# Merging weight pieces of seven-product pairs, two raw buffers plus one by stage, and a seventh seven-pair in an attention kernel

## The chip, the cores and the metric

The kernel runs on one core of one Trainium2 chip. The metric is device time in microseconds (us). The kernel before was timed in three runs: 2825.72, 2826.1 and 2832.35 us, with the median at 2826.1.

## The reference

Two layers on x of 512 rows (S) by 2048 columns (D), in float32, batch 1:

```python
def reference(x, c, ...):
    for l in range(2):
        mod = silu(c) @ ada_w[l] + ada_b[l]           # shift, scale, gate
        h = rmsnorm(x, g_pre[l]) * (1 + scale) + shift
        if l == 0:
            y = mlstm_mixer(h, a_w_in, ...)           # 8 heads, then @ a_w_out
        else:
            hkv = rmsnorm(x, kv_g) * (1 + kscale) + kshift
            k, v = split(hkv @ kv_w)                  # 2048 -> 2 x 2048
            y = band_attention_mixer(h, k, v, b_w_in, b_rel, b_w_out)
        x = x + gate * rmsnorm(y, g_post[l])
```

The first mixer projects h to queries, keys, values (8 heads of 512), an output gate o and a gate z, runs a gated linear attention over the heads, and multiplies by a_w_out (4096 to 2048). The second projects h to queries q and gates z for 16 heads of 128, takes a softmax over scores with a learned bias by relative position, mixes the values, multiplies by silu(z), and multiplies by b_w_out (2048 to 2048).

## The kernel before

Every large product is made as three matmuls of split operands (`mm3`, L215): each float32 value is split into a high and a low part (`split`: the high part cast on ACT, L179, the low part subtracted on DVE, L180), and TensorE (PE) adds hi x hi, hi x lo and lo x hi in PSUM (L213). Activations are kept in SBUF as such pairs. Weights are streamed in pieces, in the order of a list (`stream`), by `wpiece` (L184): one DMA on SP's queue into a tile `raw` of up to 128 x 1024 floats (`wr`, 512 KB), then `wh` on ACT and `wl` on DVE. Pool `wp` has three buffers each of raw, hi and lo. Pieces are numbered over the whole stream (wr0, wr1, ...).

`proj_s` (L255) makes two output column blocks of 128 at once, over pairs of row blocks k. A pair is handled in one of two ways. An "eight" is the plain product: 12 matmuls of 512 columns. A "seven" is one level of a Strassen-like scheme: seven products of 256 columns, 21 matmuls, for which sums of the weights are made first: `ws` in three DVE steps on raw (L199 to L201), split into `wsh` and `wsl`. It also needs sums of the activations (`half_sums`, `three_sums`), made by `head_sums` for the first layer and `input_sums` for the second. `pair_pieces(f)` sets what goes into a piece: of eight pairs, f are sevens. The first pieces hold one seven and one eight (1024 columns); the remaining sevens go one to a piece of 512 columns (256 KB), or, for kv_w, two to a piece.

The stages, in the trace's time: modulation, norm and leading projections until 240 us; heads 0 to 3 until about 820; heads 4 to 7, in which o and z are made by `proj_s` with five sevens of eight pairs, until about 1530; the product with a_w_out (`ps_y`), until about 1898; values (`ps_kv`) and keys of the second layer, with the residual of the first layer beside them, until about 2235; 16 attention heads (`queries`, `weights`, `flipped`, `mixed`) until about 2635, one every 25.46 us; the product with b_w_out (`ps_y` of y1) and the last norm. At the start of the head called HALF, the fourth counted from 0, a pool is closed and another, `hq`, opened for the sums; the values v of that head are evicted from PSUM (pool psP, 5 banks) by ACT and DVE in between.

A scheduler sets the order on each engine, by dependencies, priorities and pools. `tc.high_priority(300)` draws pieces and evictions ahead. An engine works strictly in that order, SP's DMA queue too: a DMA that waits for its buffer holds up all behind it. A new pool lies on memory of closed ones, so its first writes wait for the last readers there.

In the attention, head h's queries are made while head h-1's scores and softmax (`ps_s`, L990 to L993) and head h-2's mixing (`ps_o`, L1021) run at the point `mid`, in the middle of `proj_s`; `flipped` (`ps_t`) follows. After head 15's queries come the tails of heads 14 and 15. Each result z is stored to `y2c` in DRAM; the output stage loads it back in pairs as `y2r` into raw tiles of pool wp (L1060), splits it, and multiplies.

Of the kernel before, what the change touches and what calls it, by code (L numbers as in the profile page):

```python
# [15 lines left out]
P = 128  # L16
# [16 lines left out]
AHEAD = 300  # L33

# [8 lines left out]
HEAD_PAIRS = 5  # L43
HALF = NH // 2
ATT_PAIRS = 6


def pair_pieces(f, step=1):


    sk, nk = list(range(f)), list(range(f, KT // 2))
    n = min(len(sk), len(nk))
    out = [([a], [b]) for a, b in zip(sk, nk)]
    out[1:1] = [([], nk[i : i + 2]) for i in range(n, len(nk), 2)]
    return out + [(sk[i : i + step], []) for i in range(n, len(sk), step)]


def stream():
# [14 lines left out]
    def tile_s(mat, c1, c2, f, step=1):  # L73
        for sk, nk in pair_pieces(f, step):
            blocks = [(2 * k + i, c, P) for i, c in ((0, c1), (0, c2), (1, c2), (1, c1)) for k in sk]
            out.append((mat, blocks + [(2 * k + i, c, P) for k in nk for i in range(2) for c in (c1, c2)]))
# [6 lines left out]
    for h in range(NH):  # L83
# [7 lines left out]
        if h >= HALF:  # L91
            for i in range(4):
                tile_s("a_w_in", O0 + h * DV + i * P, Z0 + h * DV + i * P, HEAD_PAIRS)
# [11 lines left out]
    for i in range(KT // 2):  # L105
        tile_s("kv_w", 2 * i * P, (2 * i + 1) * P, KEY_PAIRS[i], 2)
# [24 lines left out]
def hybrid_trunk(ctx, tc, xT, xN, c, adaT, cols, wst, wg, ext, kc, out):  # L131
# [50 lines left out]
    ahead = [0]  # L182

    def wpiece(mat, ns=0, pl=None, bufs=2):  # L184
# [7 lines left out]
        with tc.high_priority(ahead[0]):  # L192
            raw = wp.tile([P, 1024], F32, tag="raw", name=f"wr{i}")[:, :n]
            nc.sync.dma_start(raw, wst[at : at + P * n].rearrange("(p n) -> p n", p=P))
            out = []
            if ns:
                w = ns * P
                t = pl.tile([P, 3 * w], F32, tag="ws", name=f"ws{i}", bufs=2)
                nc.vector.tensor_tensor(t[:, : 2 * w], raw[:, w : 3 * w], raw[:, : 2 * w], op=ALU.subtract)  # L199
                nc.vector.tensor_tensor(raw[:, w : 2 * w], t[:, w : 2 * w], raw[:, :w], op=ALU.add)  # L200
                nc.vector.tensor_tensor(t[:, 2 * w :], raw[:, 3 * w : 4 * w], raw[:, w : 2 * w], op=ALU.subtract)  # L201
# [3 lines left out]
            if ns:  # L205
                sh = pl.tile([P, 3 * w], F32R, tag="wsh", name=f"wsh{i}", bufs=bufs)
                sl = pl.tile([P, 3 * w], F32R, tag="wsl", name=f"wsl{i}", bufs=bufs)
                split(sh, sl, t)
                return hi, lo, sh, sl
        return hi, lo  # L210
# [9 lines left out]
    def proj(mat, xs, pss, nk, k0, k1, last, t0=0, t1=S, first=None):  # L220

        g = len(pss)
        for ka in range(k0, k1, nk):
            hi, lo = wpiece(mat)
# [9 lines left out]
    def proj_b(mat, xs, pss, ms=range(4), kts=KT, at={}, late=0):  # L234
# [3 lines left out]
        for k0 in range(0, kts, 2):  # L238
            if k0 in at:
                at[k0]()  # L240
            held.append((k0, *wpiece(mat)))
# [13 lines left out]
    def proj_s(mat, xs, ss, f, z1, z2, name, pl, bufs, at={}, step=1):  # L255
# [3 lines left out]
        pieces = pair_pieces(f, step)  # L259
        begun = set()  # L260
        h0, h1_ = slice(0, 256), slice(256, 512)
        for i, (sk, nk) in enumerate(pieces):
            if i in at:
                at[i]()
            ns = len(sk)
            parts = wpiece(mat, ns, pl, bufs)

            def acc(ps, cols, b, x, last):
                start = id(ps) not in begun
                begun.add(id(ps))  # L270
                hi, lo = parts[:2] if b >= 0 else parts[2:]
                w0 = (b if b >= 0 else b + 3 * ns) * P
                w = slice(w0, w0 + P)
                mm3(ps[:, cols], hi[:, w], lo[:, w], x[:, 0, :], x[:, 1, :], start, last)

            def eight():
                for m, k in enumerate(nk):
                    for j in range(2):
                        for t, ps in enumerate((A, B)):
                            acc(ps, slice(0, S), 4 * ns + 4 * m + 2 * j + t, xs[2 * k + j], False)  # L280

            def seven():
                end = i == len(pieces) - 1
                for ps, cols, b0, x, last in (
                    (D, h1_, ns, lambda k: ss[k][1], False),
                    (D, h0, 0, lambda k: xs[2 * k][:, :, h0], end),
                    (C, h0, -2 * ns, lambda k: ss[k][2], False),
                    (C, h1_, -3 * ns, lambda k: ss[k][0], end),
                    (A, h0, 3 * ns, lambda k: xs[2 * k + 1][:, :, h0], False),
                    (A, h1_, -ns, lambda k: xs[2 * k + 1][:, :, h1_], end),  # L290
                    (B, h0, 2 * ns, lambda k: ss[k][3], end),
                ):
                    if i == 0 and ps is B:
                        eight()
                    for j, k in enumerate(sk):
                        acc(ps, cols, b0 + j, x(k), last and j == ns - 1)
# [3 lines left out]
            seven()  # L300
# [60 lines left out]
    sp = st.enter_context(pool("start"))  # L361
# [100 lines left out]
    bp = mst.enter_context(pool("ada1", side="right"))  # L462
# [110 lines left out]
    def pair(c, name):  # L573
        z1, z2 = (acp.tile([P, 2, 256], F32, tag="so", name=f"{name}_{i}", bufs=6) for i in range(2))
        proj_s("a_w_in", h1, h1s, HEAD_PAIRS, z1, z2, name, hq, 2)
# [32 lines left out]
    for h in range(NH):  # L608
# [49 lines left out]
        if h == HALF:  # L658
            head_sums()
# [87 lines left out]
    rp = rst.enter_context(pool("rp", bufs=12, side="right"))  # L747
# [151 lines left out]

    with tc.high_priority(AHEAD):  # L900
        residual(2)
        residual(3)
    for pair, ms in enumerate(PAIRS):
        for g in range(2):
# [3 lines left out]
            values(g, ms, turn)  # L908
    rst.close()
# [233 lines left out]
```

## Time and profile before

| what | number |
| --- | --- |
| profiled execution, its own time | 2828.65 us |
| its span | 2826.9 us |
| mean granted PE clock | 0.997 |
| median of three runs (lowest, highest) | 2826.1 us (2825.72, 2832.35) |
| weight loads of 512 KB, 384 KB, 256 KB | 466, 16, 138 |
| PE, DVE, ACT busy, share of the span | 99%, 73%, 47% |

In the rows that are quoted below, a timeline row gives the start in us, the length in us, the engine, the line, the operation, output and inputs, shape, and a count (x2: two in a row, merged). A bracket at the end tells how long the engine stood idle before, and what ended it. Starts are what to subtract: lengths of pipelined matmuls overlap. PEclk is the clock that was granted to PE, as a share of the full one. A waits row gives the total, the number of times and the longest.

### The profile page before, as it was taken

How to read it: one execution, taken by the hardware profiler on the slowest of the kernel's cores; microseconds unless marked ns; L12 is line 12 of the kernel's file. 1: busy time of each engine (PE TensorE's matmuls, PEld its weight loads, DVE VectorE, ACT ScalarE, POOL GpSimd, SP SyncE). 2: the span in 40 equal slices, each digit the busy share in tenths (PEclk: the TensorE clock that was granted, in tenths of full speed). 3: DMA queues.
4: the chain of work that ended last, by engine and by line, in shares of the span. 5: the costliest groups of instructions: out<-in, count | busy, mean ns of one | idle time of the engine just before them, and what ended most of it. 6: DMA issues, size and time to landing. Idle time of an engine off the chain costs nothing.

```text
span 2826.9 us, 40577 instructions
## 1 busy us (share of the span) xinstructions
PE 2788.7 (99%) x15173; PEld 2417.6 (86%) x15173; DVE 2050.1 (73%) x3668; ACT 1337.0 (47%) x2040; POOL 0.2 (0%) x4
## 2 busy tenths in 40 slices
PE   7999999999999999999999999999999999999998
PEld 5787888888888989989888888888998899999887
DVE  7986978878688776766857445567985688888625
ACT  4234524234234554544635344468534466666523
POOL 0000000000000000000000000000000000000000
PEclk9999999999999999999999999999999999999999
DMA  8875687878774332332323656788535534334634
GB/s 296 300 256 179 230 313 237 298 237 282 263 245 136 98 125 85 105 105 97 116 86 135 217 198 212 251 264 283 176 130 186 157 120 128 118 126 124 222 110 171
DMA packets 184606, 524.09 MB, mean 185 GB/s; under 512 B 19620, under 2 KB 37060, under 8 KB 183896
## 3 DMA queue, kind: packets, MB, share of 16 engines
q1 hardware_dynamic: 184408, 521.49, 55.1%
q8 instruction: 119, 1.95, 0.3%
q14 instruction: 79, 0.65, 0.1%
HBM read 487.81 MB, written 38.85 MB: 186 GB/s over the span
## 4 chain that ended last, share of the span: by engine, by line
PE 89%; DVE 4%; DMA 3%; ACT 2%; issue 1%; SPq 0%; DVEq 0%; ACTq 0%
PE ps_y L213 17%; PE ps_v L213 10%; PE ps_o L213 6%; PE ps_z L213 5%; PE ps_azo L213 4%; PE ps_qk L213 4%; PE ps_az L213 4%; PE ps_kv L213 4%; PE ps_l L213 3%; PE ps_bzo L213 3%; PE ps_bz L213 3%; PE ps_dz L213 2%; PE ps_cz L213 2%; PE ps_s L213 2%; PE ps_czo L213 2%; PE ps_dzo L213 2%
## 5 line engine op out<-in xcount | busy, mean ns | idle before, releaser
L179 ACT CAST wh<-wr 128x1024 fp32r<-128x1024 f32 (+3 forms) x640 | 595.8, 932 | 833.3 <-PE ps_y L213 230.3
L180 DVE TENSOR_TENSOR wl<-wr,wh 128x1024 fp32r<-128x1024 f32 (+3 forms) x640 | 687.4, 1075 | 390.2 <-ACT wh L179 384.3
L213 PE MATMUL ps_y<-wh,y 128*128 128x512 f32 x1536 | 475.9, 390 | 0.0
L213 PEld LDWEIGHTS ps_y<-wh,y 128*128 128x128 f32 x1536 | 288.3, 188 | 59.3
L213 PE MATMUL ps_v<-wh,h 128*128 128x512 f32 x1024 | 321.7, 390 | 0.0
L179 ACT CAST wsh<-ws 128x384 fp32r<-128x384 f32 (+1 forms) x238 | 131.1, 551 | 356.3 <-issue 171.1
L213 PE MATMUL ps_y<-wl,y 128*128 128x512 f32 x768 | 299.3, 390 | 0.0
L180 DVE TENSOR_TENSOR wsl<-ws,wsh 128x384 fp32r<-128x384 f32 (+1 forms) x238 | 143.3, 603 | 154.1 <-ACT wsh L179 154.0
L213 PEld LDWEIGHTS ps_v<-wh,h 128*128 128x128 f32 x1024 | 192.3, 188 | 40.3 <-DVE zq L306 0.9
L213 PE MATMUL ps_v<-wl,h 128*128 128x512 f32 x512 | 199.9, 390 | 0.0
L370 DVE CUSTOM_DVE_ANT_0 ada<-ada,scB,cl 128x1024 f32<-128x1024 f32 x128 | 163.9, 1281 | 23.4 <-DMA ada<-in_adaT 23.2
L370 DVE CUSTOM_DVE_ANT_0 ada<-ada,scB,mod 128x1024 f32<-128x1024 f32 x128 | 164.0, 1281 | 21.6 <-DMA ada<-in_adaT 20.1
L213 PEld LDWEIGHTS ps_y<-wl,y 128*128 128x128 f32 x768 | 144.2, 188 | 29.9 <-DVE wl L180 0.5
L213 PE MATMUL ps_kv<-wh,hkv 128*128 128x512 f32 x512 | 160.6, 393 | 1.0 <-ACT wh L179 1.0
L199 DVE TENSOR_TENSOR ws<-wr 128x256 f32<-128x256 f32 (+1 forms) x238 | 106.1, 452 | 35.3 <-DMA wr<-in_wst 34.1
L213 PE MATMUL ps_qk<-h,wh 128*128 128x512 f32 x384 | 119.1, 390 | 0.0
L213 PE MATMUL ps_o<-h,wh 128*128 128x512 f32 x384 | 118.3, 389 | 0.0
L213 PE MATMUL ps_z<-h,wh 128*128 128x512 f32 x384 | 118.2, 389 | 0.0
L213 PEld LDWEIGHTS ps_kv<-wh,hkv 128*128 128x128 f32 x512 | 96.6, 189 | 21.1 <-ACT wh L179 1.4
L213 PEld LDWEIGHTS ps_v<-wl,h 128*128 128x128 f32 x512 | 96.2, 188 | 19.7 <-issue 0.9
L213 PE MATMUL ps_l<-h,wh 128*128 128x512 f32 x320 | 99.1, 391 | 2.5 <-ACT oz L456 2.0
L213 PE MATMUL ps_kv<-wl,hkv 128*128 128x512 f32 x256 | 100.6, 393 | 0.8 <-DVE wl L180 0.8
(385 smaller groups left out, 5865.3 us busy)
## 6 DMA issues: line engine op xcount, KB each, us to landing
wr<-in_wst SPq DMA_DIRECT2D x466, 512.0 KB, 4.0
ada<-in_adaT SPq DMA_DIRECT2D x256, 512.0 KB, 5.9
wr<-in_wst SPq DMA_DIRECT2D x138, 256.0 KB, 2.7
xt<-nsc SPq DMA_DIRECT2D x44, 256.0 KB, 4.1
yr<-ysc SPq DMA_DIRECT2D x16, 512.0 KB, 4.3
wr<-in_wst SPq DMA_DIRECT2D x16, 384.0 KB, 5.4
bsc<-in_ext SPq DMA_DIRECT2D x16, 320.0 KB, 5.7
xt<-in_xT SPq DMA_DIRECT2D x4, 1024.0 KB, 7.1
```

What stands on the lines that cost most here:

```text
L179: nc.scalar.copy(hi, src)
L180: nc.vector.tensor_tensor(lo, src, hi.bitcast(F32), op=ALU.subtract)
L199: nc.vector.tensor_tensor(t[:, : 2 * w], raw[:, w : 3 * w], raw[:, : 2 * w], op=ALU.subtract)
L213: nc.tensor.matmul(ps, a, b, start=start, stop=stop)
L370: pin(nc.vector.tensor_tensor_reduce(at, at, scB[:, j * D // 2 : (j + 1) * D // 2], 1.0, mod[:, i : i + 1] if j else col(CB + i), ALU.mult ...
```

## The change

The numbers of pieces fall. `pair_pieces` puts two remaining sevens into one piece of 1024 columns, as two groups with sums of their own (`ws545_0`, `ws545_1`), where it put one into 512 columns; kv_w keeps its wide group. ATT_PAIRS goes from 6 to 7, so a head's queries take 4 pieces where they took 6, and `mid` is at piece 2. Raw tiles of pool wp are two in place of three. Every third piece (its number divisible by three) takes a third raw tile in a pool that belongs to the stage, `spare[0]`: at the start `sp`, then `bp`, none from HALF to head 7, then `rp` for the first output product and the values, none for keys and attention, and pool `x2` in the output stage. `wsh` and `wsl` of the first layer have three buffers. The first pair of HALF has four sevens (RAMP), and the fifth `head_sums` moves from behind the values to piece 1 of that pair. The residual of rows 2 and 3 loses its high priority. Over the program PE's order has 8446 matmuls of 512 columns for 8626, and 6210 of 256 for 5895.

```diff
+RAW_BUFS = 2
...
+RAMP = [4, 5, 5, 5]
 HALF = NH // 2
-ATT_PAIRS = 6
+ATT_PAIRS = 7
...
     sk, nk = list(range(f)), list(range(f, KT // 2))
-    n = min(len(sk), len(nk))
-    out = [([a], [b]) for a, b in zip(sk, nk)]
-    out[1:1] = [([], nk[i : i + 2]) for i in range(n, len(nk), 2)]
-    return out + [(sk[i : i + step], []) for i in range(n, len(sk), step)]
+    n = len(nk)
+    assert n <= f
+    out = [([[a]], [b]) for a, b in zip(sk, nk)]
+    return out + [([sk[i : i + 2]] if merged else [[k] for k in sk[i : i + 2]], []) for i in range(n, f, 2)]
...
-            raw = wp.tile([P, 1024], F32, tag="raw", name=f"wr{i}")[:, :n]
+            own = spare[0] and i % (RAW_BUFS + 1) == 0
+            raw = (spare[0] if own else wp).tile([P, 1024], F32, tag="raw", name=f"wr{i}", bufs=1 if own else RAW_BUFS)[:, :n]
...
+            for j, ns in enumerate(groups):
                 w = ns * P
-                t = pl.tile([P, 3 * w], F32, tag="ws", name=f"ws{i}", bufs=2)
...
+                r = raw[:, c0 : c0 + 4 * w]
+                t = pl.tile([P, 3 * w], F32, tag="ws", name=f"ws{i}_{j}", bufs=tbufs)
...
-    sp = st.enter_context(pool("start"))
+    sp = spare[0] = st.enter_context(pool("start"))
...
-    bp = mst.enter_context(pool("ada1", side="right"))
+    bp = spare[0] = mst.enter_context(pool("ada1", side="right"))
...
+            spare[0] = None
             mst.close()
...
-        if h == HALF:
-            head_sums()
...
-                o, sz = pair_oz = pair(O0 + h * DV + i * P, f"zo{h}_{i}")
+                f = HEAD_PAIRS if h > HALF else RAMP[i]
+                o, sz = pair(O0 + h * DV + i * P, f"zo{h}_{i}", f, {1: head_sums} if len(h1s) == f < HEAD_PAIRS else {})
...
-    rp = rst.enter_context(pool("rp", bufs=12, side="right"))
+    rp = spare[0] = rst.enter_context(pool("rp", bufs=12, side="right"))
...
-                raw = wp.tile([P, 2, S], F32, tag="raw", name=f"yr{h}_{q}")
+                raw = wp.tile([P, 2, S], F32, tag="raw", name=f"yr{h}_{q}", bufs=RAW_BUFS)
...
-    with tc.high_priority(AHEAD):
-        residual(2)
-        residual(3)
+    residual(2)
+    residual(3)
...
+    spare[0] = None
     rst.close()
...
-        proj_s("b_w_in", h2, h2s, ATT_PAIRS, z[:, 0:2, :], z[:, 2:4, :], f"z{h}", kq, 3, {3: mid})
+        proj_s("b_w_in", h2, h2s, ATT_PAIRS, z[:, 0:2, :], z[:, 2:4, :], f"z{h}", kq, 3, {2: mid})
...
-    rp = ost.enter_context(pool("x2", bufs=8))
+    rp = spare[0] = ost.enter_context(pool("x2", bufs=8))
...
-            raw = wp.tile([P, 2, S], F32, tag="raw", name=f"y2r{i}")
+            raw = wp.tile([P, 2, S], F32, tag="raw", name=f"y2r{i}", bufs=RAW_BUFS)
```

The order of the instructions moves at three places. The first is DVE at the start of head 4 (HALF), around the eviction of its first block of values, v4_0, out of PSUM. h1r4 and h1s4 belong to the fifth head_sums, h1r3 and h1s3 to the fourth. Before:

```order
L569 TENSOR_TENSOR h1r4_0_6900<-h1_8_929 128x512
L319 TENSOR_TENSOR h1r3_1_6816<-h1r3_1_6816 128x256
L180 TENSOR_TENSOR h1s3_0_6822<-h1r3_0_6814,h1s3_0_6822 128x512
L316 TENSOR_TENSOR h1r4_0_6900<-h1r4_0_6900 128x256
L180 TENSOR_TENSOR h1s3_1_6825<-h1r3_1_6816,h1s3_1_6825 128x512
L569 TENSOR_TENSOR h1r4_1_6902<-h1_9_971 128x512
L180 TENSOR_TENSOR v4_0_6914<-ps_v4_0_6544,v4_0_6914 128x512
L180 TENSOR_TENSOR wl180_7032<-wr180_7025,wh180_7031 128x1024
```

And now:

```order
L182 TENSOR_TENSOR v4_0_6900<-ps_v4_0_6544,v4_0_6900 128x512
L182 TENSOR_TENSOR h1s3_1_6825<-h1r3_1_6816,h1s3_1_6825 128x512
L206 TENSOR_TENSOR ws181_0_7074<-wr181_7072 128x256
L615 TENSOR_TENSOR e4_0_6703<-e4_0_6703,p4_3_6867 128x128
L207 TENSOR_TENSOR wr181_7072<-ws181_0_7074,wr181_7072 128x128
L182 TENSOR_TENSOR v4_1_6903<-ps_v4_1_6545,v4_1_6903 128x512
L182 TENSOR_TENSOR wl180_7032<-wr180_7025,wh180_7031 128x1024
L208 TENSOR_TENSOR ws181_0_7074<-wr181_7072 128x128
L182 TENSOR_TENSOR v4_2_6906<-ps_v4_2_6546,v4_2_6906 128x512
L182 TENSOR_TENSOR wsl181_0_7083<-ws181_0_7074,wsh181_0_7082 128x384
L580 TENSOR_TENSOR h1r4_0_6964<-h1_8_929 128x512
L580 TENSOR_TENSOR h1r4_1_6966<-h1_9_971 128x512
```

The first steps of h1r4 stood ahead of v4_0 and wl180; now they stand behind v4_0, v4_1, v4_2, wl180 and the sums of piece 181.

The second is DVE at the start of the values (the first piece is 424 before and 402 now, so 430 before is 408 now). y3_2 and y3_3 are the residual's last steps; they read xr3_2 and xr3_3, which come by DMA. Before:

```order
L180 TENSOR_TENSOR wl428_16158<-wr428_16155,wh428_16157 128x1024
L779 RECIPROCAL rsn_106<-rsn_106 128x1
L789 SCALAR_TENSOR_TENSOR y3_2_15622<-y3_2_15622,rsn_106,xr3_2_16066 128x512
L180 TENSOR_TENSOR wl429_16176<-wr429_16173,wh429_16175 128x1024
L789 SCALAR_TENSOR_TENSOR y3_3_16017<-y3_3_16017,rsn_106,xr3_3_16072 128x512
L777 TENSOR_REDUCE rsn_106<-ssq_105 128x1
L180 TENSOR_TENSOR wl430_16194<-wr430_16191,wh430_16193 128x1024
```

And now:

```order
L800 SCALAR_TENSOR_TENSOR y3_1_15174<-y3_1_15174,rsn_106,xr3_1_15911 128x512
L182 TENSOR_TENSOR wl407_16027<-wr407_16024,wh407_16026 128x1024
L182 TENSOR_TENSOR wl408_16045<-wr408_16042,wh408_16044 128x1024
L182 TENSOR_TENSOR wl409_16063<-wr409_16060,wh409_16062 128x1024
L182 TENSOR_TENSOR wl410_16121<-wr410_16118,wh410_16120 128x1024
L800 SCALAR_TENSOR_TENSOR y3_2_15473<-y3_2_15473,rsn_106,xr3_2_15917 128x512
L800 SCALAR_TENSOR_TENSOR y3_3_15868<-y3_3_15868,rsn_106,xr3_3_15923 128x512
L182 TENSOR_TENSOR wl411_16139<-wr411_16136,wh411_16138 128x1024
```

The low parts of pieces 408 to 410 stood behind y3_3 (as 430 to 432); now they stand ahead of y3_2.

The third is the change from the attention to the output stage. On PE, ps_t14, ps_o14, ps_s15 belong to the tails of heads 14 and 15, and ps_y1_0 is the first row of the output product. Before, from the end of head 14's transposes:

```order
L213 MATMUL ps_y1_0_0_24928<-wl600_24935,y2_0_0_24940 128x512
L213 MATMUL ps_y1_0_0_24928<-wh600_24934,y2_0_0_24940 128x512
L213 MATMUL ps_y1_0_1_24929<-wh600_24934,y2_0_0_24940 128x512
L213 MATMUL ps_y1_0_1_24929<-wl600_24935,y2_0_0_24940 128x512
L1003 MATMUL ps_t14_3_24807<-kcs_99,s14_3_24658 128x128
L213 MATMUL ps_y1_0_1_24929<-wh600_24934,y2_0_0_24940 128x512
L213 MATMUL ps_y1_0_0_24928<-wh600_24934,y2_0_1_24943 128x512
L213 MATMUL ps_y1_0_2_24930<-wh600_24934,y2_0_0_24940 128x512
L213 MATMUL ps_o14_24814<-pt14_0_24791,vv14_24811 128x512 x3
L213 MATMUL ps_o14_24814<-pt14_1_24798,vv14_24811 128x384
L213 MATMUL ps_y1_0_2_24930<-wl600_24935,y2_0_0_24940 128x512
L213 MATMUL ps_y1_0_2_24930<-wh600_24934,y2_0_0_24940 128x512
```

And now, at the same place:

```order
L1014 MATMUL ps_t14_2_24748<-kcs_99,s14_2_24573 128x128
L1014 MATMUL ps_t14_2_24748<-kcs_99,s14_3_24582 128x128
L1014 MATMUL ps_t14_3_24754<-kcs_99,s14_3_24582 128x128
L223 MATMUL ps_o14_24761<-pt14_0_24738,vv14_24758 128x512 x3
L223 MATMUL ps_o14_24761<-pt14_1_24745,vv14_24758 128x384 x3
L223 MATMUL ps_o14_24761<-pt14_2_24751,vv14_24758 128x256 x3
L223 MATMUL ps_s15_0_24775<-kv15_24082,z15_24423 128x128
L223 MATMUL ps_o14_24761<-pt14_3_24756,kv14_23741 128x128
L223 MATMUL ps_s15_1_24782<-k15_24727,q15_24723 128x256 x3
```

The matmuls of ps_y1_0 have gone from between the tails' steps. The first of them, which reads wh546, now stands right behind the last matmul of ps_o15.

On SP at the same place, y2c7 are the stores of the results of heads 14 and 15, y2r the loads of results, x2 the loads of the residual for the last norm. Before:

```order
L194 DMA wr602_25008<-in_wst 128x1024
L1060 DMA y2r2_25014<-y2c2_92 128x1024
L194 DMA wr603_25046<-in_wst 128x1024
L1060 DMA y2r3_25052<-y2c3_93 128x1024
L1022 DMA y2c7_97<-z14_24148 128x512
L194 DMA wr604_25084<-in_wst 128x1024
L1060 DMA y2r4_25090<-y2c4_94 128x1024
L194 DMA wr605_25122<-in_wst 128x1024
L1060 DMA y2r5_25128<-y2c5_95 128x1024
L194 DMA wr606_25160<-in_wst 128x1024
L1022 DMA y2c7_97<-z15_24481 128x512
```

And now:

```order
L1033 DMA y2c7_97<-z15_24423 128x512
L199 DMA wr546_24879<-in_wst 128x1024
L1062 DMA x2_0_0_24858<-xsc_74 128x1024
L1062 DMA x2_0_1_24859<-xsc_74 128x1024
L1062 DMA x2_1_0_24862<-xsc_74 128x1024
L199 DMA wr549_24993<-in_wst 128x1024
L1062 DMA x2_1_1_24863<-xsc_74 128x1024
L1062 DMA x2_2_0_24866<-xsc_74 128x1024
L1062 DMA x2_2_1_24867<-xsc_74 128x1024
L1062 DMA x2_3_0_24870<-xsc_74 128x1024
L199 DMA wr552_25107<-in_wst 128x1024
L1062 DMA x2_3_1_24871<-xsc_74 128x1024
```

wr546 is the first piece of the output stage, in its own raw tile; it stands behind the store of z15, and so do wr549, wr552 and the x2 loads, behind which the loads y2r2 and y2r3 follow. Pieces 547 and 548 and the loads y2r0 and y2r1 stand ahead of the stores.

More of the change, by code (lines that the diff above doesn't have):

```diff
@@ L204, in wpiece @@
             split(hi, lo, raw)
-            if ns:
-                sh = pl.tile([P, 3 * w], F32R, tag="wsh", name=f"wsh{i}", bufs=bufs)
-                sl = pl.tile([P, 3 * w], F32R, tag="wsl", name=f"wsl{i}", bufs=bufs)
+            out = [(hi, lo)]
+            for j, t in enumerate(ts):
+                sh = pl.tile(list(t.shape), F32R, tag="wsh", name=f"wsh{i}_{j}", bufs=bufs)
+                sl = pl.tile(list(t.shape), F32R, tag="wsl", name=f"wsl{i}_{j}", bufs=bufs)
                 split(sh, sl, t)
-                return hi, lo, sh, sl
-        return hi, lo
+                out.append((sh, sl))
+        return out
     def mm(ps, a, b, start, stop):
@@ L223, in proj @@
         for ka in range(k0, k1, nk):
[L224 removed]
+            [(hi, lo)] = wpiece(mat)
             for k in range(ka, ka + nk):
```

84 lines of the change are left out of this document (44 added, 40 removed).

## Prediction

> **What bounds the kernel now.** I read the page's engine totals, then the chain that ended last, then the windows with a low granted clock, then the timeline around each of PE's waits.
>
> ```profile
> span 2826.9 us, 40577 instructions
> PE 2788.7 (99%) x15173; PEld 2417.6 (86%) x15173; DVE 2050.1 (73%) x3668; ACT 1337.0 (47%) x2040; POOL 0.2 (0%) x4
> ...
> PE 89%; DVE 4%; DMA 3%; ACT 2%; issue 1%; SPq 0%; DVEq 0%; ACTq 0%
> ```
>
> TensorE is busy 2788.7 of 2826.9 us and holds 89% of the chain. The time can fall only by less matmul time or by fewer PE waits, 38.2 us in all. It rises wherever something new makes PE wait. A wait also costs more than its length. The next rows give a window's us, then busy time of PE, its weight loads, DVE, ACT and POOL, then the granted clock:
>
> ```profile
> 898.00:904.00 6.00, 5.23 (x19) 4.81 (x20) 4.49 (x9) 2.23 (x4) 0.00 (x0) 0.50 0.25 90
> ...
> 1908.00:1910.00 2.00, 2.00 (x7) 1.52 (x6) 1.23 (x1) 0.68 (x2) 0.00 (x0) 0.50 0.78 248
> ...
> 2251.00:2639.00 388.00, 387.67 (x2770) 364.26 (x2770) 335.51 (x902) 249.82 (x488) 0.00 (x0) 1.00 0.40 124
> ```
>
> Behind PE's waits near 898 and 1906 us the clock is 0.50. In the attention, the last row, it is 1.00 and PE is idle for 0.33 us in 388.
>
> **The matmul work: -3.7 and +0.2.** In the attention's PE timeline a seven (21 matmuls of 256 columns) runs from 2272.84 to 2275.36, an eight (12 of 512) from 2281.02 to 2283.77:
>
> ```profile
> 2272.84 0.40 PE L213 MATMUL ps_dz<-h2s,wh 128*128 128x256 f32 x2
> ...
> 2275.36 0.40 PE L213 MATMUL ps_dz<-h2s,wh 128*128 128x256 f32 x2
> ...
> 2281.02 0.63 PE L213 MATMUL ps_az<-h,wh 128*128 128x512 f32 x2
> ...
> 2283.77 0.40 PE L213 MATMUL ps_bz<-h2s,wh 128*128 128x256 f32 x2
> ```
>
> That is 2.52 us (0.120 a matmul) against 2.75 (0.229). One more seven in each of 16 heads gives 16 x 0.23 = 3.7 us less; RAMP turns one seven back into an eight, +0.2. The whole programs agree: 180 matmuls of 512 columns fewer (-41.2) and 315 of 256 more (+37.8) make -3.4. PE does not wait there, so this term is safe.
>
> **The start of head 4: -2 (0 to -4).** PE's rows first, then two of DVE's:
>
> ```profile
> 893.44 0.40 PE L213 MATMUL ps_dzo<-h1s,wh 128*128 128x256 f32 x2
> ...
> 898.77 0.80 PE L213 MATMUL ps_dzo<-h1s,wh 128*128 128x256 f32 x2 [3.73 <-ACT wh L179]
> ...
> 904.76 0.40 PE L213 MATMUL ps_azo<-h,wh 128*128 128x512 f32 x1
> ...
> 898.05 0.69 DVE L569 TENSOR_TENSOR h1r<-h 128x512 f32<-128x512 f32 x1
> 898.65 0.69 DVE L180 TENSOR_TENSOR v<-ps_v,v 128x512 fp32r<-128x512 f32 x1
> ```
>
> From 893.44 to 904.76, 11.3 us, PE does 26 matmuls of 256 columns and 8 of 512, 4.9 us at the rates above. So 6.4 us are lost: 3.7 of wait, 2.7 of half clock behind it. DVE, busy without a break, evicts v4_0 only at 898.65, behind the first steps of the fifth head_sums (two of L569, one of L316, 1.5 us). These move behind the eviction. Against that, the sums of whole pieces come ahead. I take -2: the 1.5 and a little of the half clock. If another step is just as late, it is 0; for more than -4 the clock must hardly drop.
>
> **The start of the values: -3 (0 to -3.9).**
>
> ```profile
> 1903.33 0.75 DVE L789 SCALAR_TENSOR_TENSOR y<-y,rsn,xr 128x512 f32<-128x512 f32 x1 [2.29 <-DMA xr<-in_xN]
> ...
> 1904.52 0.39 PE L213 MATMUL ps_kv<-wh,hkv 128*128 128x512 f32 x1
> ...
> 1905.88 0.49 PE L213 MATMUL ps_kv<-wh,hkv 128*128 128x512 f32 x1 [0.97 <-ACT wh L179]
> ...
> 1907.14 0.50 PE L213 MATMUL ps_kv<-wl,hkv 128*128 128x512 f32 x1 [0.77 <-DVE wl L180]
> ...
> 1911.12 0.62 PE L213 MATMUL ps_kv<-wh,hkv 128*128 128x512 f32 x2
> ```
>
> DVE stands 2.29 us at a residual step for the transfer of xr, and ACT's next square waits for that; the casts and splits of the next weights queue behind both, and xr's loads stand in SP's queue before the weights. From 1904.52 to 1911.12, 6.6 us, PE does 12 matmuls of 512, 2.7 us: 3.9 lost. Now the splits of pieces 408 to 410 stand ahead of the two last residual steps (the order shown above), so PE's weights come first. What is late instead is the residual, due only when x is turned, some pieces later. I take -3 of the 3.9.
>
> **Small new waits: +1.7 (0 to +10).** The rows: PE's wait at the first keys, the last ps_n of head 7 and the first ps_y behind it, then DVE's waits for transfers and its groups in the attention:
>
> ```profile
> 2007.72 0.50 PE L213 MATMUL ps_ak<-hkv,wh 128*128 128x256 f32 x2 [0.94 <-DVE zk L306]
> ...
> 1527.03 5.59 PE L213 MATMUL ps_n<-p,v 128*128 128x512 f32 x33
> 1532.38 0.48 PE L213 MATMUL ps_y<-wh,y 128*128 128x512 f32 x1
> ...
> DVE ws L199 <- DMA wr<-in_wst: 0.5, 1, 0.5
> ...
> L180 DVE TENSOR_TENSOR wsl<-ws,wsh 128x384 fp32r<-128x384 f32 x90 | 49.9, 555 | 32.3 <-ACT wsh L179 32.3
> ...
> L199 DVE TENSOR_TENSOR ws<-wr 128x256 f32<-128x256 f32 x88 | 36.7, 418 | 0.5 <-DMA wr<-in_wst 0.5
> L201 DVE TENSOR_TENSOR ws<-wr 128x128 f32<-128x128 f32 x89 | 25.5, 287 | 0.5
> L200 DVE TENSOR_TENSOR wr<-ws,wr 128x128 f32<-128x128 f32 x88 | 25.1, 286 | 0.5
> ```
>
> - Keys: DVE's queue grows by one group's sums and splits (up to 0.418 + 0.286 + 0.287 + 0.555 = 1.5 us) ahead of the bank that PE waits for, so its 0.94 us may grow; I take +0.7 (0 to +2).
> - First output rows: the stage's own buffer lies on memory that head 7's last pair still reads, and can be loaded from about 1527. It carries the second piece, and the 5.6 us of ps_n and the first piece's 24 matmuls (5.5 us) cover a load and a split. I take +0.5 (0 to +3).
> - Attention: those same 1.5 us in each of some 25 us a head take DVE from 335.51/388.00 = 86% to about 92%. DVE's waits there are for ACT (32.3 us) and hardly for transfers (0.5 us). With two raw buffers for what were three, a transfer may now end a wait. I take +0.5 in all, ends 0 and +5 (a third of a us a head).
>
> The third buffer at the start and in heads 0 to 3 replaces one of the same size: nothing, since there are three either way. In heads 4 to 7 it is missing, with whole pieces; their waits lie in the ends above.
>
> **From attention to output: +19.5 (+12 to +24.5).** This is the term that decides. Rows: the start of head 14's transposes, which ends head 15's queries on PE, the first y1 matmul, the last of ps_o15, then DVE, ACT and SP; then the page's two rows of weight transfers with their median us to landing:
>
> ```profile
> 2634.84 1.14 PE L1003 MATMUL ps_t<-kcs,s 128*128 128x128 f32 x9
> 2635.74 0.48 PE L213 MATMUL ps_y<-wh,y 128*128 128x512 f32 x1
> ...
> 2653.56 0.39 PE L213 MATMUL ps_o<-pt,kv 128*128 128x128 f32 x2
> 2653.70 0.48 PE L213 MATMUL ps_y<-wh,y 128*128 128x512 f32 x1
> ...
> 2647.23 1.22 DVE L180 TENSOR_TENSOR wl<-wr,wh 128x1024 fp32r<-128x1024 f32 x1
> ...
> 2648.44 0.68 DVE L180 TENSOR_TENSOR y<-y2r,y 128x512 fp32r<-128x512 f32 x1
> 2649.03 0.48 DVE L993 TENSOR_SCALAR s<-s,mx 128x512 f32<-128x512 f32 x1
> ...
> 2653.44 1.04 ACT L179 CAST wh<-wr 128x1024 fp32r<-128x1024 f32 x1
> ...
> 2655.66 0.68 DVE L1021 TENSOR_TENSOR z<-ps_o,z 128x512 f32<-128x512 f32 x1
> ...
> 2657.36 0.43 SPq L1022 DMA_DIRECT2D y2c<-z  x1
> ...
> wr<-in_wst SPq DMA_DIRECT2D x466, 512.0 KB, 4.0
> ...
> wr<-in_wst SPq DMA_DIRECT2D x138, 256.0 KB, 2.7
> ```
>
> From 2634.84 on, only head 14's and 15's tails are left of the attention: transposes, softmax, two mixings, a chain across PE, DVE and ACT. PE has no idle in these 18.9 us, because 48 matmuls of y1's first two pieces lie between its steps, 48 x 0.229 = 11.0 us. After the change PE's order has none there: y1's first matmul stands behind the last of ps_o15. And its weights, wr546, are the first load into the output stage's own buffer, on the attention's memory: SP issues it behind both y2c7 stores, the second of which needs ps_o15 and a DVE step.
>
> The chain's end: 2653.70 before. DVE then also ran splits of y and of weights on the way, which go (up to 5.3 us: two of 1.14 and five of 0.6, start to start); PE's steps at half clock add up to 3. I take 2651.5, ends 2648.4 and 2654.5. From there the DVE step 0.7, the store's issue 0.4, the load 4.0 and the cast 1.0 make 6.1: y1 starts at 2657.6. Had the 48 matmuls of before been put behind the chain, y1 would start at 2653.70 - 11.0 = 2642.7. So 14.9 us are lost (11.8 to 17.9).
>
> Then the clock: PE will have idled longer than the 3.73 us at 898, after which the half clock cost 2.7; I take +2.6 (0 to 2.7). The Trainium skill (TensorE: Matmul & The Clock Gate, Part 1, What's actually happening) puts the clock at half after an idle window of about 3.4 us, until about as long a busy one. By it the restart costs about 1.7 us, an estimate, and the term would be 0.9 less; the trace's 0.50 over all of 898 to 904 is longer, and near 1908 it came after waits of 0.97 and 0.77 us alone.
>
> Last, y2r2, which the third piece needs, is queued on SP behind eight x2 loads and two weight loads, one of which (wr552) waits until the first piece's buffers are free: 5.5 us of matmuls, then cast, split, load and split again, about 5.5 + 2.2 + 4.0 + 1.2 = 12.9 us after y1's start, against two pieces, 10.9: +2 (0 to 4). Sum 14.9 + 2.6 + 2 = 19.5.
>
> **The rivals.** (a) The tail is cheap and the change is faster. Where the chain of head 15 ended at 2638.6, with 6.1 us behind it, y1 would start by 2644.7, 2 us lost, and the sum is -3.5 - 4 - 3.9 + 2 = -9.4: 2816.7 on the median. It decides from a y1 start before about 2645.6. For it: PE never idles there before, so the records don't show the chain's bare length. Against it: s15's last scaling stands at 2649.03 and depends on every step before. Chance 0.10.
>
> (b) Gains and losses nearly cancel. The chain shrinks to 2648.4, y2r2 comes in time and the clock recovers at once: +11.8, and the starts give back their -4 and -3.9: with -3.5 and +1.7 it is +2.1, 2828. Chance 0.24.
>
> (c) The attention starves as well. If each head waits 1 us for a transfer or DVE, 16 us come on top: 2854. For it: 86% grows to about 92%, 4.0 us transfers into two buffers. Against it: DVE still has some 2 us a head, and PE's idle there is only 0.33 us so far. Chance 0.08. The Trainium skill speaks for this one (Perfetto Trace Analysis, DMA Optimizations): where DMA engines are mostly idle, transfers split smaller may let some start sooner; the change joins them. The attention's DMA share of 0.40 fits its condition; its waits for transfers, 0.5 us, do not yet show the harm.
>
> (d) That the change does not do what it says: the counts of matmuls rule it out.
>
> **How the numbers follow.** Sum: -3.7 + 0.2 - 2 - 3 + 1.7 + 19.5 = +12.7. Against the profiled run's own 2828.65 us (its span 2826.9 and 1.75 around it) that is 2841.4. That run was 2.55 above the median of the three, 2826.1; on the median it is 2838.8, and I give 2838. A measurement of this kernel tells about 0.3%, 8.5 us, from no change: faster is below 2817.6, slower above 2834.6. My forecast has 0.58; with (c), slower has 0.66, same 0.24, faster 0.10. The range, 2822 to 2850, leaves out (a) and nearly all of (c) and holds the ends of the last term with the others near their middle.
>
> **What would show it.** Right: PE idle 12 us or more between 2630 and 2660, its first ps_y of y1 behind the last ps_o, released by ACT wh, with the clock near 0.5; heads of about 25.2 us in the attention; no wait of wl on xr near 1905. Wrong: ps_y between ps_t and ps_o; y1 started within 4 us of the chain's end; or new waits of PE in every head, each next to a transfer.

## The result and the profile after

The changed kernel takes 2851.78 us (median of 6 runs, 2849.18 to 2855.48), the kernel before 2825.64 in the runs beside it (2823.32 to 2832.35): a ratio of 1.0091 with a 95% interval of 1.0078 to 1.0104, 26.1 us more. The direction was forecast; the forecast size was 12.7 us, and the time lies 1.8 us above the range.

The page of the changed kernel, the same rows as before:

```profile
span 2852.6 us, 40697 instructions
...
PE 2796.1 (98%) x15308; PEld 2425.8 (85%) x15308; DVE 2074.9 (73%) x3680; ACT 1337.4 (47%) x2005; POOL 0.2 (0%) x4
...
PE 86%; DVE 6%; DMA 4%; ACT 2%; issue 1%; SPq 0%; DVEq 0%; ACTq 0%
```

The span grew by 25.7 us. PE's busy time grew too, though its matmuls should take 3.4 us less: matmuls at half clock count as busy. To find the place I cut PE's timeline where one stage's matmuls give way to the next one's, and took the differences of starts. In us, one profiled execution each:

| stage, up to | before | changed | difference |
| --- | --- | --- | --- |
| heads 0 to 3, last ps_qk | 845.75 | 846.49 | +0.7 |
| head 4 | 137.96 | 137.17 | -0.8 |
| heads 5 to 7, first ps_y | 548.67 | 547.97 | -0.7 |
| first output, first ps_kv | 356.05 | 355.68 | -0.4 |
| first values, last ps_kv there | 94.72 | 91.61 | -3.1 |
| keys, next ps_kv | 164.57 | 170.46 | +5.9 |
| second values | 87.07 | 87.07 | 0.0 |
| attention, last ps_bz | 399.92 | 400.49 | +0.6 |
| tails and output, last ps_y | 182.40 | 205.69 | +23.3 |

They add up to the 25.5 us between the two last matmuls. How far one execution can be trusted shows when the kernels below are counted in whose code in a stretch is the changed kernel's: the keys took 167.5 to 170.5 us in six profiles, the attention 399.0 to 401.0 in six, tails and output 204.6 to 207.0 in four. So the end gave 23.3, as the largest of the waits shows. These are the changed kernel's rows of PE's waits, with total, times and longest:

```profile
PE ps_y L223 <- ACT wh L181: 6.0, 1, 6.0
PE ps_y L223 <- ACT y L181: 4.6, 1, 4.6
...
PE ps_ak L223 <- DVE zk L317: 2.4, 1, 2.4
...
PE ps_ck L223 <- DVE zk L314: 1.8, 1, 1.8
```

The end in PE's timeline, and in windows (us, then busy time of PE, weight loads, DVE, ACT, POOL, then the granted clock):

```profile
2637.06 1.15 PE L1014 MATMUL ps_t<-kcs,s 128*128 128x128 f32 x9
...
2645.78 2.09 PE L1014 MATMUL ps_t<-kcs,s 128*128 128x128 f32 x9 [1.52 <-DVE s L1004]
...
2652.83 0.63 PE L223 MATMUL ps_o<-pt,kv 128*128 128x128 f32 x2
2659.41 1.22 PE L223 MATMUL ps_y<-wh,y 128*128 128x512 f32 x2 [5.95 <-ACT wh L181]
...
2677.83 0.56 PE L223 MATMUL ps_y<-wh,y 128*128 128x512 f32 x1 [4.65 <-ACT y L181]
```

```profile
2634.00:2654.00 20.00, 14.76 (x80) 11.63 (x79) 11.87 (x33) 10.21 (x23) 0.00 (x0) 0.84 0.12 41
2644.00:2647.41 3.41, 1.71 (x10) 0.90 (x9) 2.83 (x13) 2.11 (x8) 0.00 (x0) 1.00 0.21 77
2654.00:2660.00 6.00, 0.59 (x1) 0.50 (x2) 0.80 (x2) 1.69 (x2) 0.00 (x0) 0.50 0.80 247
2660.00:2666.00 6.00, 5.96 (x18) 4.25 (x17) 2.89 (x3) 1.25 (x2) 0.00 (x0) 0.63 0.96 358
2661.07:2664.48 3.41, 3.41 (x9) 2.64 (x9) 1.82 (x2) 0.18 (x1) 0.00 (x0) 0.50 0.95 358
2664.48:2667.89 3.41, 3.41 (x16) 2.78 (x16) 0.00 (x0) 0.11 (x1) 0.00 (x0) 1.00 0.98 371
```

The first ps_y of y1 stands behind the last ps_o. PE waits 5.95 us for its weights, and 4.65 us more at the third piece for y2r2. The clock falls to 0.50 already in the tails, at 2647.41, behind 3.41 us in which PE worked for 1.71, and comes back at 2664.48, 5.07 us after y1's start.

### The profile page after: what moved, and what is told of

The parts are those of the page before. It is cut to its first block, busy times and chain, and to the rows that moved or that the text cites. A ratio compares the mean times of both kernels' runs of the same rounds, so it can differ in the third digit from the quotient of the medians.

```text
span 2852.6 us, 40697 instructions
## 1 busy us (share of the span) xinstructions
PE 2796.1 (98%) x15308; PEld 2425.8 (85%) x15308; DVE 2074.9 (73%) x3680; ACT 1337.4 (47%) x2005; POOL 0.2 (0%) x4
## 4 chain that ended last, share of the span: by engine, by line
PE 86%; DVE 6%; DMA 4%; ACT 2%; issue 1%; SPq 0%; DVEq 0%; ACTq 0%
PE ps_y L223 18%; PE ps_v L223 10%; PE ps_o L223 5%; PE ps_z L223 5%; PE ps_azo L223 4%; PE ps_qk L223 4%; PE ps_kv L223 4%; PE ps_bzo L223 3%; PE ps_az L223 3%; PE ps_l L223 3%; PE ps_cz L223 2%; PE ps_dz L223 2%; PE ps_czo L223 2%; PE ps_dzo L223 2%; PE ps_s L223 2%; PE ps_bz L223 2%
## 5 line engine op out<-in xcount | busy, mean ns | idle before, releaser
L181 ACT CAST wh<-wr 128x1024 fp32r<-128x1024 f32 (+3 forms) x586 | 585.1, 1000 | 860.0 <-PE ps_y L223 210.0
L182 DVE TENSOR_TENSOR wl<-wr,wh 128x1024 fp32r<-128x1024 f32 (+3 forms) x586 | 678.5, 1160 | 421.5 <-ACT wh L181 416.7
L181 ACT CAST wsh<-ws 128x384 fp32r<-128x384 f32 (+1 forms) x253 | 138.4, 547 | 321.5 <-issue 127.3
L182 DVE TENSOR_TENSOR wsl<-ws,wsh 128x384 fp32r<-128x384 f32 (+1 forms) x253 | 151.5, 599 | 99.8 <-ACT wsh L181 98.3
L381 DVE CUSTOM_DVE_ANT_0 ada<-ada,scB,cl 128x1024 f32<-128x1024 f32 x128 | 163.7, 1280 | 25.7 <-DMA ada<-in_adaT 25.6
L381 DVE CUSTOM_DVE_ANT_0 ada<-ada,scB,mod 128x1024 f32<-128x1024 f32 x128 | 163.9, 1280 | 19.9 <-DMA ada<-in_adaT 18.4
L206 DVE TENSOR_TENSOR ws<-wr 128x256 f32<-128x256 f32 (+1 forms) x253 | 112.2, 451 | 34.9 <-DMA wr<-in_wst 31.8
L223 PEld LDWEIGHTS ps_kv<-wh,hkv 128*128 128x128 f32 x512 | 95.7, 188 | 19.5
```

Source lines behind the costliest of these rows:

```text
L181: nc.scalar.copy(hi, src)
L182: nc.vector.tensor_tensor(lo, src, hi.bitcast(F32), op=ALU.subtract)
L206: nc.vector.tensor_tensor(t[:, : 2 * w], r[:, w : 3 * w], r[:, : 2 * w], op=ALU.subtract)
L223: nc.tensor.matmul(ps, a, b, start=start, stop=stop)
L381: pin(nc.vector.tensor_tensor_reduce(at, at, scB[:, j * D // 2 : (j + 1) * D // 2], 1.0, mod[:, i : i + 1] if j else col(CB + i), ALU.mult ...
```

## Experiments on the end

Each kernel below is the changed kernel with one edit, unless its heading says otherwise. Where there is one run, its whole time lies too near the changed kernel's 2849.18 to 2855.48 us to decide much by itself, so the stretches of the table are compared.

### out_two: no raw buffer of its own in the output stage

```diff
-    rp = spare[0] = ost.enter_context(pool("x2", bufs=8))
+    rp = ost.enter_context(pool("x2", bufs=8))
+    spare[0] = None
```

> The changed kernel, but with no raw buffer of its own in the output stage (two raw buffers there). Theory A, that the 23 us at the end come from the first output piece being put into the stage's own buffer on the attention's memory: PE has output matmuls between the tails' steps again, the first ps_y stands before the last ps_o, and the time falls by about 20 us to about 2832. Rival B, that two raw buffers in place of three are the cause, wherever the first piece lies: the wait for y2r or wr stays, and the time falls by less than 8 us.

Measured: 2844.14 us, a ratio of 1.0058 (1.0041 to 1.0076). Tails and output take 194.00 us, 11.7 less than in the changed kernel and 11.6 more than before. PE has output matmuls in the tails again. But this stands in PE's timeline at the fifth piece:

```profile
2672.78 0.79 PE L223 MATMUL ps_y<-wh,y 128*128 128x512 f32 x1 [5.33 <-ACT y L181]
```

Theory A's signs came, but not its 20 us: the fall is 7.6 us between the two medians, about 9 by the two ratios, and 11.7 in the stage. Rival B's sign came too, a wait for y2r, and its bound of 8 us is neither clearly kept nor broken. The first piece's place explains about half of the 23 us. Of the other 11.6, 5.33 are the wait for y2r, which in this kernel's order too stands on SP behind x2 loads; half clock goes with it (0.50 from 2670.72 to 2677.55), and four waits of 2.5 us in all stand at the end of the output.

### x2_late: the x2 loads behind the first row of output products

The loads of x2 become a function, called when the first of the four column groups is done. The first piece stays in its own buffer. In the order that comes of it on SP, three of the eight x2 loads still go out ahead of y2r2.

```diff
-    for m in range(4):
-        t = [rp.tile([P, 2, S], F32, tag="x2", name=f"x2_{m}_{i}") for i in range(2)]
+    def residual_rows():
+        for m in range(4):
+            t = [rp.tile([P, 2, S], F32, tag="x2", name=f"x2_{m}_{i}") for i in range(2)]
...
+        if g == 0:
+            residual_rows()
```

> The changed kernel, with the x2 loads created behind the first row of output products instead of ahead of it, so that y2r2 stands earlier in the DMA queue. The first piece's own buffer stays. Theory A: the first wait of 6.0 us stays, and the second, 4.65 us for y2r2, goes with the half clock behind it: 4 to 6 us less in the output stage. Rival: y2r2 waits for its buffer and not for its place in the queue; then the second wait stays.

Measured: one run, 2846.29 us. Tails and output take 199.66 us, 6.0 less. No wait stands behind the first one, whose row is nearly unchanged; the windows show the clock recover once and stay at 1.00:

```profile
2657.57 1.22 PE L223 MATMUL ps_y<-wh,y 128*128 128x512 f32 x2 [6.01 <-ACT wh L181]
```

```profile
2658.00:2664.00 6.00, 5.96 (x19) 4.27 (x19) 3.04 (x3) 1.41 (x2) 0.00 (x0) 0.69 0.95 348
2664.00:2678.00 14.00, 14.00 (x63) 11.59 (x62) 6.24 (x8) 5.42 (x8) 0.00 (x0) 1.00 0.91 318
```

So y2r2's place in the queue cost 6.0 us: 4.65 of wait and some 1.4 of half clock behind it. In the changed kernel SP issued y2r2 at 2670.97, behind a weight load that went out 7.2 us after the x2 loads before it; here at 2659.93, 2.4 us after y1's start.

### out_fix: both edits

```diff
-    rp = spare[0] = ost.enter_context(pool("x2", bufs=8))
+    rp = ost.enter_context(pool("x2", bufs=8))
+    spare[0] = None
...
+        if g == 0:
+            residual_rows()
```

> The changed kernel without a raw buffer of its own in the output stage, and with the x2 loads created behind the first row of output products. From the end of head 15's queries to the last matmul: 182.4 us before, 205.7 changed, 194.0 with the first of the two edits alone, 199.7 with the second alone. If the place of x2 in the queue is what is left: 183 to 186 us and a time of about 2834. If two raw buffers shared by weights and y2r are: 190 us or more, a time of 2840.

Measured: 2838.64 us, 1.0045 (1.0028 to 1.0062). Tails and output take 188.18 us, between the two expectations, 5.8 us above before. These are all of PE's waits from 2630 us on:

```profile
PE ps_y L223 <- ACT wh L181: 1.3, 2, 0.9
PE ps_y L223 <- DVE wl L182: 1.1, 2, 0.8
PE ps_y L223 <- ACT y L181: 0.9, 1, 0.9
PE ps_y L223 <- ACT sqy L783: 0.4, 1, 0.4
```

Four of the six, 2.3 of the 3.6 us, stand from 2811 us on, where the last pieces come late to two raw buffers. The other 2.2 of the 5.8 us are in no wait row. So two causes shared the 23.3 us, the first piece's buffer and the place of y2r behind x2, and this kernel pays anew for having only two raw buffers. The third buffer comes back in the last kernel, best552.

## Experiments on the keys, the values and the attention

### kx_own: a third raw buffer for the keys

```diff
+    xst = ExitStack()
+    spare[0] = xst.enter_context(pool("kx", side="right"))
     for i in range(KT // 2):
...
+    spare[0] = None
+    xst.close()
     kst.close()
```

> The changed kernel, with a third raw buffer in a pool of its own while the keys are made. Theory C, that the keys lose 5.9 us because two raw buffers let DVE wait for weights (2.00 us at 1982): the two PE waits near 2003 and 2007 (1.8 and 2.4 us) fall below 1.5 us together, the clock stays at 1.00, and from the end of the first values to the second values PE takes at least 4 us less than in the changed kernel. Rival D, that the residual, moved back, and one more sums step weigh on DVE: the waits stay within 1 us of what they are.

The changed kernel's rows at the keys: a stand of DVE for weights, the two waits of PE, and the window behind them.

```profile
1982.01 0.42 DVE L206 TENSOR_TENSOR ws<-wr 128x256 f32<-128x256 f32 x1 [2.00 <-DMA wr<-in_wst]
...
2003.37 0.51 PE L223 MATMUL ps_ck<-hs,wsh 128*128 128x256 f32 x2 [1.83 <-DVE zk L314]
...
2006.71 0.79 PE L223 MATMUL ps_ak<-hkv,wh 128*128 128x256 f32 x2 [2.37 <-DVE zk L317]
...
2007.00:2013.00 6.00, 6.00 (x19) 4.94 (x19) 5.67 (x10) 1.80 (x2) 0.00 (x0) 0.54 0.40 145
```

Measured: one run, 2850.97 us; the keys take 164.36 us, against 170.46 changed and 164.57 before. With the third buffer, over 1975 to 2010, DVE's wait for weights is the first row below (2.8 us in the changed kernel), and PE's only wait near 2005 the second:

```profile
DVE ws L206 <- DMA wr<-in_wst: 1.2, 2, 1.0
```

```profile
2004.90 0.50 PE L223 MATMUL ps_ak<-hkv,wh 128*128 128x256 f32 x2 [0.58 <-DVE zk L317]
...
2005.00:2013.00 8.00, 8.00 (x56) 7.50 (x57) 8.00 (x14) 3.38 (x4) 0.00 (x0) 1.00 0.40 141
```

Theory C holds: with the third buffer the keys are back at what they took before. DVE runs behind by about the 2 us it stood at 1982, reaches the sums of zk that much later, and PE waits for the banks. The clock then adds to the bill: the two waits are 3.3 us longer than the 0.94 of before, and the keys lost 5.9.

What makes the clock fall shows when the windows are cut where it changes. In all twelve profiles it is 1.00 or 0.50 and nothing else, and the changes within a run lie whole multiples of 3.41 us apart. Four such steps of the changed kernel, then the one around the 0.94 us of the kernel before:

```profile
2002.29:2005.70 3.41, 0.98 (x6) 0.77 (x6) 2.73 (x7) 2.25 (x4) 0.00 (x0) 1.00 0.08 31
2005.70:2009.12 3.42, 2.41 (x9) 2.22 (x10) 3.42 (x8) 0.00 (x0) 0.00 (x0) 0.50 0.45 153
2009.12:2012.53 3.41, 3.41 (x10) 2.64 (x9) 3.41 (x6) 1.80 (x2) 0.00 (x0) 0.50 0.46 163
2012.53:2015.94 3.41, 3.41 (x28) 3.32 (x27) 1.62 (x3) 1.05 (x1) 0.00 (x0) 1.00 0.37 144
...
2006.56:2009.97 3.41, 2.48 (x15) 2.02 (x15) 3.41 (x8) 2.94 (x4) 0.00 (x0) 1.00 0.39 142
```

Parts of both waits fall into the first step, in which PE works 0.98 us, and the clock halves at its end; it comes back behind the third, which PE fills. Over the twelve profiles, from 40 us on to 10 us before the end, every step at full clock with 1.9 us or more of idle PE was followed by half clock, and none with less than 1.3. Between the two it went both ways. So the idle time within a step counts here, not the length of one wait.

### res_high: the residual at high priority again

```diff
-    residual(2)
-    residual(3)
+    with tc.high_priority(AHEAD):
+        residual(2)
+        residual(3)
```

> The changed kernel with the residual of rows 2 and 3 at high priority again. All theories: the waits of PE at the start of the values come back, about 3 us. Theory C: the keys' waits near 2003 and 2007 stay, 4 us together. Rival D: they fall to about the 1 us of the kernel before.

Measured: one run, 2855.39 us. The values take 93.98 us (91.61 changed), and the keys 169.25. All waits of PE from 1890 to 2012:

```profile
PE ps_ak L223 <- DVE zk L317: 2.4, 1, 2.4
PE ps_ck L223 <- DVE zk L314: 2.2, 1, 2.2
PE ps_x L829 <- DVE xn L821: 0.9, 1, 0.9
PE ps_kv L223 <- DVE wl L182: 0.8, 1, 0.8
```

The waits at the keys stay, so the residual's place is not their cause. The values lose 2.4 us again.

### before_res: the kernel before, with only the residual's priority taken away

```diff
-    with tc.high_priority(AHEAD):
-        residual(2)
-        residual(3)
+    residual(2)
+    residual(3)
```

> The kernel before with one part of the change alone: the residual of rows 2 and 3 loses its priority. The prediction's step for the start of the values: the two PE waits at 1905.9 and 1907.1 and the half clock behind them go, 3 us less from the first to the last ps_kv of the first values (94.7 us before, 91.6 in the changed kernel), and the keys stay at 164.6 us; the time falls by about 3 us. Rival: with three raw buffers the weights are there anyway and the values start late for another reason; 94 us as before.

Measured: 2823.23 us against 2827.34 beside it, 0.9988 (0.9978 to 0.9997). The values take 90.78 us, the keys 162.99. PE's waits from 1890 to 2012 are one row:

```profile
PE ps_ak L213 <- DVE zk L306: 0.6, 1, 0.6
```

The keys were expected at 164.6 and came 1.6 lower. This one line of the change is a gain by itself: 3.9 us in the values, as the rows of before had bounded it.

### att6: six sevens in the attention, still two to a piece

```diff
-ATT_PAIRS = 7
+ATT_PAIRS = 6
```

> The changed kernel with six sevens of eight pairs in the attention, still two sevens to a piece. Attention here is from the end of the second values to the last matmul of head 15's queries: 399.9 us before, 400.5 in the changed kernel, against 396.2 by the count of matmuls. Theory E, that DVE's added work for the seventh seven ate what PE saved: the attention takes 400 us within 0.7, so the seventh seven is worth nothing. Theory F, that the merged transfers and two raw buffers delay DVE: the waits stay and the attention takes about 404 us.

Measured: one run, 2855.41 us; the attention takes 400.83 us. That is 0.1 outside theory E's 400 within 0.7, and far from theory F's 404. PE has no wait at all there, while it has 1.5 us with seven. Before, with the same matmuls in smaller pieces, it took 399.92, and 399.27 in before_res, so the 0.9 us that the merged pieces seem to cost is hardly more than what two profiles of the same code differ by. From 400.83, the seventh seven should give 397.1.

### att_act: the softmax's scaling on ACT

```diff
-            nc.vector.tensor_scalar(s, s, r, None, op0=ALU.mult)
+            nc.scalar.activation(s, s, AF.Identity, scale=r)
```

> The changed kernel, with the four scalings of the softmax (s by its row's reciprocal) on ACT in place of DVE, about 1.2 us of DVE less a head. Theory E (DVE's load): PE's waits for DVE in the attention go and the attention falls from 400.5 to 396 to 398 us. Theory F (transfers): it stays at 400 us or more. The tail of heads 14 and 15 may move by 1 us either way.

Measured: one run, 2864.64 us; the attention takes 407.91 us, 7.4 more. Theory E's 396 to 398 did not come. Theory F's 400 or more did, but the edit also gives ACT 2.1 us of scalings a head in the place of 1.5 on DVE, so this run alone decides neither. Over 2251 to 2632, DVE's busy time went from the first row's 346.28 to the second's 323.95 us, yet PE's fell as well:

```profile
2251.00:2632.00 381.00, 379.40 (x2852) 362.28 (x2852) 346.28 (x923) 245.27 (x461) 0.00 (x0) 1.00 0.37 123
```

```profile
2251.00:2632.00 381.00, 375.22 (x2801) 355.45 (x2800) 323.95 (x846) 265.57 (x504) 0.00 (x0) 1.00 0.37 120
```

What grew are stands of DVE, for ACT and for bias. The changed kernel's rows first, then this kernel's:

```profile
DVE wl L182 <- ACT wh L181: 15.1, 19, 2.0
DVE wsl L182 <- ACT wsh L181: 8.2, 14, 0.7
DVE bias L984 <- DMA bias<-bsc: 5.8, 9, 1.5
```

```profile
DVE wl L182 <- ACT wh L181: 25.4, 43, 2.0
DVE bias L984 <- DMA bias<-bsc: 15.3, 13, 2.4
DVE mx L1003 <- ACT s L1002: 8.8, 12, 0.8
DVE wsl L182 <- ACT wsh L181: 3.1, 13, 0.2
```

### bias_pool: the mask of bias on GpSimd

In `queries`, DVE overwrites a corner of bias (a memset of 0.11 us), once bias has landed. It stood nowhere for that before. In the changed kernel's DVE order the memset comes sooner: for one of the last heads it ran 16.0 us after the load's issue before (first row, the load issued at 2603.22), and 5.3 now (second row, issued at 2603.50), with 0.56 us of standing.

```profile
2619.22 0.11 DVE L973 MEMSET bias<- 64x64 f32 x1
...
2608.83 0.11 DVE L984 MEMSET bias<- 64x64 f32 x1 [0.56 <-DMA bias<-bsc]
```

```diff
-        nc.vector.memset(bias[:64, 448:512], NEG)
+        nc.gpsimd.memset(bias[:64, 448:512], NEG)
```

> The changed kernel, with the mask written into bias by GpSimd in place of DVE, so that DVE no longer stands for the transfer of bias (5.8 us in nine waits between 2251 and 2632). Theory G, that this stand is what makes DVE late: the attention falls from 400.5 to 398 us or less. Theory E: it falls by less than 1.5 us.

Measured: one run, 2846.61 us; the attention takes 397.63 us, 2.9 less, and DVE is as busy as ever:

```profile
2251.00:2632.00 381.00, 380.23 (x2871) 364.78 (x2869) 347.98 (x909) 245.86 (x465) 2.46 (x14) 1.00 0.38 122
```

Theory G's number came, and with DVE as busy as before, theory E's cause is out. PE's 1.5 us of waits in the attention are gone; the other 1.4 of the 2.9 us are in no wait row. The six profiles with DVE's memset took 399.0 to 401.0 us there, 400.1 on average, this one and best552 397.63 both. So DVE at 91% does not starve PE here; DVE standing in its queue for a transfer does.

### best552: the repairs together

The changed kernel with kx_own, bias_pool and x2_late, and with the stage's own buffer in the output from its seventh piece on only:

```diff
-            own = spare[0] and i % (RAW_BUFS + 1) == 0
+            own = spare[0] and i % (RAW_BUFS + 1) == 0 and not 546 <= i < OUT0
```

> The changed kernel with all that the runs so far pointed to: a third raw buffer of its own pool while the keys are made, the mask of bias on GpSimd, the x2 loads behind the first row of output products, and the output stage's own raw buffer used only from its seventh piece on (552). By the sums of the stages: keys 164.5 us (170.5 changed), attention 397.6 (400.5), from the end of the queries to the last matmul 184 to 188 (205.7, and 182.4 before). Together about 2824 us, 0 to 5 us below the kernel before. If the first pieces of the output stage need the third raw buffer that they had before, the last stretch takes 188 us or more, and the time is that of before or up to 4 us above.

Measured: 2823.2 us (11 runs) against 2827.34 beside it, 0.9985 (0.9976 to 0.9993). Keys 165.21, attention 397.63, tails and output 182.90 us, where it was 182.40 before. That last is below the expected 184 to 188: a third buffer for the later pieces took away the waits of out_fix. PE is full through the tails, with its clock at 1.00, and y1 begins right behind head 14's transposes:

```profile
2629.34 1.15 PE L1019 MATMUL ps_t<-kcs,s 128*128 128x128 f32 x9
2630.24 0.47 PE L224 MATMUL ps_y<-wh,y 128*128 128x512 f32 x1
```

```profile
2629.00:2649.00 20.00, 20.00 (x109) 16.43 (x108) 16.26 (x39) 14.98 (x30) 0.00 (x0) 1.00 0.42 152
```

It beats the kernel before by 0.15%, about as much as before_res does with one line. That line is in this kernel too, so the rest of the change has no gain to show.

## Why the prediction was right and wrong

**Right: the term that decides, and its mechanism.** From the end of head 15's queries the start of y1 was put at 2657.6 - 2634.84 = 22.8 us; it came at 2659.41 - 2637.06 = 22.35. The chain was put at 16.7 us and ended at about 16.4 (2653.5), and the 6.1 us from there to y1 were 5.95. The loss of 14.9 us, taken the same way, was 14.5. out_two, x2_late and best552 show the cause: the buffer of the first piece and the queue order that comes with it. One detail was otherwise: the clock did not fall with the wait for y1's weights but 12 us before y1, in the tails.

**Wrong in size: y2r2, +2.** The step had y2r2 land 2 us late. It came 4.65 us late, and the step had left out the second fall of the clock: 6.0 us together, by x2_late. Put at 12.9 us from y1's start to the split y2r2, it took 18.4: the weight load ahead of it went out after 10.7 us (taken 7.7), and y2r2 needed 6.2 us to land (taken 4.0). The first restart cost what is left of 23.3, 2.8 us (taken +2.6); half clock for 5.07 us after y1's start makes 2.5. The term came to 23.3 in place of 19.5, within its end of 24.5.

On the rule that was weighed there (the Trainium skill, TensorE: Matmul & The Clock Gate, Part 1, What's actually happening): its window of about 3.4 us fits the 3.41 us between the clock's steps here. But the clock fell behind a step in which PE still worked for 1.71 us, so no whole idle window was needed. And the restart came within a step: 5.07 us of half clock here, 4.19 in x2_late (2657.57 to 2661.76), where the estimate of 1.7 us had counted 3.4.

**Failed: the keys, +0.7 (0 to +2).** They cost 5.9. The step counted one group's work on DVE and forgot the buffer: `spare[0]` is None there, so the keys run on two raw tiles where they had three. kx_own returns the whole of it. And two waits of 1.83 and 2.37 us, 1 us of work between them, were enough to halve the clock for 6.83 us; a wait of 0.94 before was not. The prediction itself had the row for that, at 1908, and did not use it here.

**Failed: the attention's waits, +0.5 (0 to +5).** The stage was put at -3.7 + 0.5 and measured +0.6, so 3.8 us more were lost than forecast, 4.3 with the 0.5 that was taken: 2.9 by the stand for bias (bias_pool). The other 1.4 stay open; 0.9 of them stand in att6 against before too, in no wait row and hardly beyond the scatter. The end of +5 held. The cause that the step named, a wait for weights into two buffers, is in no run: DVE never waits for wr there. So rival (c) had the place and a wait for a transfer right, but the wrong transfer, and 16 us for 3.8. The rule on splitting transfers that stood beside it (the Trainium skill, Perfetto Trace Analysis, DMA Optimizations) finds no support in the attention: with the pieces joined, DVE's waits for wr went from 0.5 us to none.

**Right: the values, -3.** Measured -3.1; res_high and before_res give 2.4 and 3.9 for the same line.

**Undecided: head 4, -2 and +0.2.** Measured -0.8. Ten profiles of kernels that are equal up to there took 135.0 to 139.4 us in this stretch, more scatter than the term. Most of the scatter is the clock: behind much the same waits, half clock lasted 0 us in one (135.0), 3.41 in four (136.4 to 137.2) and 6.83 in five (137.5 to 139.4). The order did what was said, since the wait moved from wh to the evictions of v (2.27 and 1.04 us), but I can't say what that is worth.

**Right: the matmul count.** It shows only once the attention is freed: 397.63 against 400.83 with six sevens, one profile each, is -3.2, where 16 x 0.23 = 3.7 was expected.

The sum's error by the table, 25.5 - 12.7 = 12.8 us, is thus 5.2 from the keys, 3.8 from the attention and 3.8 from the end; the rest cancels. Nothing came out as rival (a) or (b) had it.

## What to carry to other kernels

Where a pool lends a buffer by stage, list for every stage how many buffers it has left, and ask which instruction first takes the borrowed one: it waits for the last reader of the memory below, and all that is queued behind waits along. At a full TensorE, work that lies between the steps of a dependent chain is worth its full length; look for it in the order of both programs before counting instructions. And before lightening a busy engine, look for what it stands for in its queue.

## What the runs showed that I had not expected

- Two waits of under 2.4 us each within 6 us halve the clock for 6.83 us (2005.70 to 2012.53), and that costs nearly as much again as the waits: 2.6 us of the 5.9 at the keys.
- The same waits cost more or less by how they fall on the clock's steps of 3.41 us: two waits of 3.3 us in all at head 4 were followed by 3.41 us of half clock in the changed kernel, and by none in bias_pool.
- Taking 22 us of work from DVE made the attention 7.4 us longer (att_act). That ACT, with 2.1 us a head more to do, is the reason is argued from DVE's longer waits for it, not shown by itself.
